# Key outputs last among the dense products, first branch-A outputs behind the attention, another deal of the sample steps

## The chip, the cores and the metric

The kernel runs on one core of one Trainium2 chip. A core has TensorE (matrix products; PE below, with PEld for its weight loads), VectorE (DVE), ScalarE (ACT), GpSimd (POOL) and SyncE (SP), which here issues DMA transfers. The engines run their own instruction lists in order and wait for one another by semaphores. The metric is the device time of one execution in microseconds. Before the change the median of three runs is 1980.49 us (1976.86 to 1985.71).

## The reference

One decoder layer is computed in float32 for two groups with shared weights: a prompt of 1024 tokens and a sample group of 8 sequences with 4 new tokens each and 8192 cached tokens in pages. The core of it:

```python
h = rmsnorm(x, g_norm1) * (1 + scale1) + shift1
za, zq, zkv, zg, zm = split(h @ w_in)              # gMLP, queries, keys/values, gates, merge gates
ya = chunk_spatial_gating(u, vn, w_spatial, b_spatial)          # u, v from gelu(za)
yb = nsa_attention(q, kv_rows, win_rows, ...)      # compressed + selected blocks + window, gated sum
gate_a, gate_b = split(sigmoid(zm))
mixed = (gate_a * (ya @ w_branch_a) + gate_b * (yb @ w_branch_b)) @ w_out
x = x + gate1 * mixed
x = x + gate2 * conv_ffn(rmsnorm(x, g_norm2) * (1 + scale2) + shift2)
```

The attention has three parts: over compressed blocks of 64 keys, over the 16 blocks that the compressed scores select, and over a window of 512 keys. The outputs are the results y of both groups, the new key and value rows (among them `o_k`, the keys of the selected and window branches), the window buffers, the normalised v rows and the rows of the convolution's state.

## The kernel before

**Numbers.** Each float32 product is made of three passes of TensorE over a high part and a low part of both operands (helper `mm`, L56; all matmuls that go through it carry this line). The parts are made by ACT (a cast, L319) and DVE (a subtraction, L320) in `split`. All columns of the layer, 1024 prompt and 32 sample tokens, stand side by side as R = 1056 columns in three chunks of 384, 384 and 288 (`CH`). `products` computes 128 output rows for one chunk: for K input tiles 3K matmuls into one PSUM bank, then an eviction.

**Stages.** Statistics of x and the tiles of h; row products; gMLP; then the dense outputs that remain, in the list `fill`: four query tiles (`query`), two key tiles (`key`; key 0 is that of the selected, key 1 of the window branch), 16 merge gates (`merge_gate`, kept in DRAM as `sig_d`). Between them stand groups of the compression of the cached pages (`compress`, 16 in all; its ACT and DVE ends are L553, L568 and L569), of which groups 14 and 15 come behind the last dense output. Tiles of 128 x 1056 live in a pool of 24 slots; h holds 16 of them until the dense outputs are done.

**The start of the attention.** `key` writes its tile to DRAM (`o_k`). `key_tiles` reads it back (L843) and makes, for each of the two heads, a high and a low part in both halves of the partitions: ACT casts (L847), DVE subtracts (L848), and DVE copies both into the other half (L849 the high, L850 the low part). `queries` makes the query parts of one tile of 128 tokens (ACT L864, DVE L865).

**The attention.** The prompt's 8 query tiles times 4 head groups are 32 units; unit n computes its scores in `attend`, the exponentials on ACT (L1136), the transposes of the probabilities on TensorE (L1161) and, two units later, `values`. The sample group's selected blocks are worked on in 32 steps between them: `sel_scores`, `sel_turn`, `sel_values`, and after every fourth step `sel_merge`, a small chain of DVE, ACT and two matmuls, which comes from `later` with a count of turns of `one_more` between its parts. Each step needs a page buffer, one of four, which SyncE fills with 16 loads of 128 KB (L522). The same four buffers take the chunks of `w_ada` (L1053; in every fourth unit) and, in two places, the weights of the near keys (L909, L911). At the end they take `ya` and `w_ba` (L1262, L1267).

**What sets the order.** Within the attention TensorE's order is the order in which the program is written (`tc.manual_schedule`), so `one_more`, `later` and the numbers that generators yield place every matmul. Other engines are ordered by the framework's scheduler. The steps are dealt to the units by `work` and `due` (L1253 and L1254): a unit's weight is an estimate of its work plus a constant, and `due[n]` is the number of steps that are to be started by unit n.

**Blocks.** `blocks` selects each sample query's compressed blocks; the part for the second group of four sequences is put on TensorE's list in unit 0. It yields the number of turns until its next part; the part behind its second yield (L794) starts with 16 small transposes of the mask, which need DVE's selection (L781 to L789).

**After the attention.** Branch A: 8 outputs, each of three products of 12 matmuls over the parts of `ya`, multiplied at the eviction (L1358) with the merge gate's tile, which SyncE loads (L1355). Their PSUM banks come from `pA`, a pool of the products; the attention uses four banks from `pM`. Then branch B, `w_out`, and the convolutional network follow.

Of the kernel before, what the change touches and what calls it, by code (L numbers as in the profile page):

```python
# [6 lines left out]
F32 = mybir.dt.float32  # L7
F32R = mybir.dt.float32r
# [3 lines left out]
OP = mybir.AluOpType  # L12
# [3 lines left out]
R = 1056  # L16
# [34 lines left out]
def step_kernel(tc, A):  # L51
# [23 lines left out]
    def pA():  # L75
        return psum([128, 512], F32, "A", 4)
# [18 lines left out]
    def slot(dt=F32):  # L95
        return S([128, R], dt, "S", NS)
# [220 lines left out]
    def split(t, hi, lo):  # L317

        act.copy(hi, t)  # L319
        dve.tensor_tensor(lo, t, hi.bitcast(F32), op=OP.subtract)  # L320
# [91 lines left out]
                lo.append(b[:, i * 128:(i + 1) * 128])  # L412
        return hi, lo

    def products(w, xh, xl, a, b, evac, behind=()):

        ps = pA()[:, 0:b - a]
        K = len(xh)
        for k in reversed(range(K)):
            with ExitStack() as queue:  # L420
                for step, ins in behind:
                    if K - 1 - k >= step:
                        queue.enter_context(tc.issue_after(ins.ins))
                mm(ps, w[0][k], xh[k][:, a:b], k == K - 1, False)
                mm(ps, w[0][k], xl[k][:, a:b], False, False)
                mm(ps, w[1][k], xh[k][:, a:b], False, k == 0)
        evac(a, b, ps)

    def dense(src, K, xh, xl, evac, load_weights=weights_t):
        w = load_weights(src, K)  # L430
        for a, b in CH:
            products(w, xh, xl, a, b, evac)
# [248 lines left out]
    def merge_gate(j, sg):  # L681
        dense(A["w_t"][10 + j], 8, hh, hl,
              lambda a, b, ps, sg=sg: act.activation(sg[:, a:b], ps, AF.Tanh, scale=0.5))  # L683
        dve.tensor_scalar(sg, sg, 0.5, 0.5, op0=OP.mult, op1=OP.add)  # L684
        stored.append(pool.dma_start(sig_d[j], sg))  # L685
        return sg
# [35 lines left out]
    def query(j):  # L722
        q = slot()
        dense(A["w_t"][4 + j], 8, hh, hl,
              lambda a, b, ps, t=q: act.mul(t[:, a:b], ps, 0.125))
        for h in range(2):
            dve.tensor_copy(QB[64 * h:64 * h + 64, :, h, :, j],
                            q[64 * h:64 * h + 64, NP:R].rearrange("p (b t) -> p b t", t=4))
        pool.dma_start(q_d[j], q)

    def key(j):
        kr = slot()
        dense(A["w_t"][8 + j], 8, hh, hl, lambda a, b, ps, t=kr: act.copy(t[:, a:b], ps))
        dve.tensor_copy(k_new[:, j], kr[:, NP:R])
        pool.dma_start(A["o_k"][j], kr)
        if j == 1:
            for b in range(8):
                pool.dma_start(A["o_wsk"][b][:, 508:512], kr[:, NP + 4 * b:NP + 4 * b + 4])
# [10 lines left out]
    def blocks(gr, bank):  # L749

        pt = bank()
        mm(pt[:, 0:24], bt_sel[0:32, gr], G[0:32, 8], True, True)
        gt = small(24, "sm24", 1).rearrange("p (a h) -> p a h", h=8)
        dve.tensor_tensor(gt, pt[:, 0:24].rearrange("p (b h) -> p b h", h=8),
                          head01[:, None, :].to_broadcast([128, 3, 8]), op=OP.mult)
        dve.tensor_reduce(GR[:, gr], gt, axis=AX.X, op=OP.add)
        g4 = small(4, "pg", 1)
        dve.tensor_scalar(g4, cg4, GR[:, gr, 1:2], None, op0=OP.mult)
        ps = bank()
        for i in range(4):  # L760
            b = 4 * gr + i
            mm(ps[32 * i:32 * i + 32, 0:128], QB[:, b].rearrange("p h t g -> p (h t g)"), kc_of(b), True, True)
        nm = small(1, "ps", 3)
        dve.tensor_reduce(nm, ps[:, 0:128], axis=AX.X, op=OP.max, negate=True)
        p = small(128, "pa", 3)
        su = small(1, "ps", 3)
        act.activation(p, ps[:, 0:128], AF.Exp, bias=nm, accum_out=su)
        r = small(1, "ps", 3)
        dve.tensor_scalar(r, su, 1e-30, None, op0=OP.max)
        dve.reciprocal(r, r)  # L770
        dve.tensor_scalar(p, p, r, None, op0=OP.mult)
        yield 3
        pt = bank()
        mm(pt[:, 0:4], rep, g4, True, True)
        dve.tensor_copy(GS[:, 4 * gr:4 * gr + 4], pt[:, 0:4])
        pt = bank()
        mm(pt[:, 0:128], grp, p, True, True)
        MA = small(128, "pa", 3)
        dve.memset(MA, 0.0)
        wk = MA[:, 1:127]  # L780
        dve.tensor_copy(wk, pt[:, 1:127])  # L781
        m8 = small(8, "m8", 2)
        dve.max(m8, wk)
        dve.match_replace(wk, m8, wk, -1.0)
        m8 = small(8, "m8", 2)
        dve.max(m8, wk)
        dve.memset(m8[:, 5:8], -5.0)
        dve.match_replace(wk, m8, wk, -1.0)
        dve.tensor_scalar(wk, wk, 0.0, NEG, op0=OP.is_ge, op1=OP.mult)  # L789
        pt = bank()  # L790
        pe.transpose(pt[:, 0:128], p, ident)
        pct = small(128, "pa", 3)
        act.copy(pct, pt[:, 0:128])
        yield 3  # L794
        pt = bank()
        for i in range(4):
            for c in range(4):
                mm(pt[32 * c:32 * c + 32, 32 * i:32 * i + 32], ident[:, 32 * i:32 * i + 32],
                   MA[:, 32 * c:32 * c + 32], True, True)
        dve.tensor_copy(MB[:, 4 * gr:4 * gr + 4], pt[:, 0:128].rearrange("p (b n) -> p b n", n=32))  # L800
        po = bank()
        for i in range(4):
            mm(po[32 * i:32 * i + 32, 0:128], pct[:, 32 * i:32 * i + 32], vc_of(4 * gr + i), True, True)
        oc = small(128, "pa", 3)
        dve.tensor_scalar(oc, po[:, 0:128], GR[:, gr, 0:1], None, op0=OP.mult)
        yield 2
        pt = bank()
        mm(pt[:, 0:128], oc, ident, True, True)
        dve.tensor_copy(YCW[:, gr], pt[:, 0:128])

    first_blocks = blocks(0, pT)

    fill = [lambda j=j: query(j) for j in range(4)] + [lambda j=j: key(j) for j in range(2)]
    fill += [lambda j=j: merge_gate(j, slot()) for j in range(16)]
    fill = iter(fill)
    R2B = new_pool("r2b")
    n = 5
# [16 lines left out]

    KH, KL = [], []

    def key_tiles(j, anchor):
        k0, k1 = slot(F32R), slot(F32R)
        l0, l1 = slot(F32R), KX([128, NP], F32R) if j else slot(F32R)
        kr = slot()  # L840
        if anchor is not None:
            dve.tensor_copy(kr[0:1, 0:1], anchor[0:1, R - 1:R])
        sync.dma_start(kr[:, 0:NP], A["o_k"][j][:, 0:NP])  # L843
        f = kr[:, 0:NP]
        for h, k, l in ((0, k0, l0), (1, k1, l1)):
            own, other = slice(64 * h, 64 * h + 64), slice(64 - 64 * h, 128 - 64 * h)
            act.copy(k[own, 0:NP], f[own])  # L847
            dve.tensor_tensor(l[own, 0:NP], f[own], k[own, 0:NP].bitcast(F32), op=OP.subtract)  # L848
            dve.tensor_copy(k[other, 0:NP], k[own, 0:NP].bitcast(F32))  # L849
            dve.tensor_copy(l[other, 0:NP], l[own, 0:NP].bitcast(F32))  # L850
        KH.append((k0, k1))
        KL.append((l0, l1))
# [13 lines left out]
        return qs  # L866


    qt = [slot() for _ in range(4)]
    for j in range(4):  # L870
        sync.dma_start(qt[j], q_d[j])
    key_tiles(0, None)
    key_tiles(1, None)
    VV = [slot(), slot()]
    for i in range(2):
        sync.dma_start(VV[i][:, 0:1024].rearrange("p (k c) -> p k c", c=256),
                       A["o_rows"][1][512 * i:512 * i + 512].rearrange("(k p) c -> p k c", p=128))

    q_first = queries(TILES[0], KL[0][0])
    for n in (14, 15):  # L880
        compress_act(*compress(n))
    compress_end()
    R2B.release()
    PG.release()
# [365 lines left out]

            later(turning(), 3)

    work = [i + 1 + min(i + 1, 5) + 6 for i, _ in units]  # L1253
    due = [max(0, 33 * sum(work[2:n + 1]) // sum(work[2:])) for n in range(len(units))] + [33] * (AHEAD + 1)  # L1254
    m = 0
    ya, ah, al = [], [], []
# [70 lines left out]
    with tc.manual_schedule(engines={mybir.EngineType.PE}):  # L1327
        later(qtile(TILES[0]), 0)
        one_more()
        for n in range(len(units) + AHEAD):  # L1330
            step(n)
        while pending:
            one_more()
    psum.release()
# [10 lines left out]


    yh, yl = [], []
    ma = []
    for m in range(8):
        w = slot(F32R)  # L1350
        split(wba[:, m], w[:, 0:512], w[:, 512:1024])
        w = [[w[:, c + 128 * k:c + 128 * k + 128] for k in range(4)] for c in (0, 512)]
        t = slot()
        dve.tensor_copy(t[0:1, 0:1], al[3].bitcast(F32)[0:1, R - 1:R])
        sync.dma_start(t, sig_d[m])  # L1355
        for a, b in CH:
            products(w, ah, al, a, b,
                     lambda a, b, ps, t=t: dve.tensor_tensor(t[:, a:b], t[:, a:b], ps, op=OP.mult))  # L1358
        ma.append(t)
    R3S.release()  # L1360
    R3.release()
    KX.release()
# [500 lines left out]
```

## Time and profile before

| | |
|---|---|
| median of the runs | 1980.49 us (1976.86, 1980.49, 1985.71) |
| profiled execution: its time | 1976.38 us |
| its span, first to last instruction | 1974.7 us |
| mean granted TensorE clock | 0.976 |
| TensorE busy | 1853.6 us |
| last dense output ends, by TensorE's row at 597.00 | 597.0 us |
| attention's first scores | 617.98 us |
| last page load issued | 995.9 us |
| branch A's first matmuls | 1019.4 us |

The profile comes from one execution. A row of the timeline has the start in us from the span's beginning, the length, the engine, the line of the kernel, the operation with its shapes, a count of instructions taken together, and in brackets the idle time of this engine ahead of it and what ended it. The granted clock is the share of TensorE's full speed that the chip's throttle allowed. SPq is SyncE's queue of DMA issues; the length there is the time of issuing, not of the transfer.

### The profile page before, as it was taken

To read this page: it belongs to the slowest core of one execution; us is meant where nothing else is said; L and a number is where in the kernel's file an instruction comes from. 1 tells how busy PE (TensorE), PEld (TensorE's weight loads), DVE (VectorE), ACT (ScalarE), POOL (GpSimd) and SP (SyncE) were. 2 spreads that over 40 slices of the span, in tenths; PEclk is the share of its full clock that TensorE was granted. 3 is DMA by queue.
4 is the path that set the end of the run, shared out by engine and by line. 5 is a ranking of instruction groups with operands and counts; after the bars stand their busy time and mean duration, and the time that the engine had idled before them with its cause. 6 is when DMAs were issued, how large, how long until landed. Compare 5 with 4: busy or idle time off the path is not lost.

```text
span 1974.7 us, 43773 instructions
## 1 busy us (share of the span) xinstructions
PE 1853.6 (94%) x16073; PEld 1746.1 (88%) x16073; DVE 1181.3 (60%) x2536; ACT 786.8 (40%) x1602; POOL 483.7 (24%) x624
## 2 busy tenths in 40 slices
PE   6799999999998998989889999799999999999996
PEld 4799999999997776767679999789999999999996
DVE  6613421112115676676665768899999999756464
ACT  4313111112114554656551357334444444545342
POOL 3410110100000000000001411766777765201010
PEclk9799999999998999999999999899999999999998
DMA  8364656766658577677773444233322223856462
GB/s 327 97 207 129 195 184 211 243 220 201 211 171 273 178 245 234 223 230 231 232 259 136 150 164 143 76 104 105 103 98 71 73 88 95 291 188 209 137 190 89
DMA packets 253894, 346.14 MB, mean 175 GB/s; under 512 B 35280, under 2 KB 189296, under 8 KB 251504
## 3 DMA queue, kind: packets, MB, share of 16 engines
q1 hardware_dynamic: 205696, 262.91, 41.3%
q10 hardware_dynamic: 36896, 41.22, 6.5%
q0 software_dynamic: 11088, 39.21, 5.6%
q8 instruction: 127, 2.08, 0.4%
q14 instruction: 87, 0.71, 0.1%
HBM read 305.96 MB, written 41.43 MB: 176 GB/s over the span
## 4 chain that ended last, share of the span: by engine, by line
PE 76%; DVE 7%; SPq 4%; issue 4%; DMA 4%; ACT 3%; POOL 1%; DVEq 0%; ACTq 0%; POOLq 0%
PE t L56 73%; SPq L522 3%; PE t L1161 2%; DMA t<-w_ada 2%; DVE t L320 1%; DMA t<-t 1%; DVE t L1583 1%; ACT t L319 1%; POOL t L1546 1%; DVE t L1523 1%; SPq L512 1%; DVE t L1522 1%; ACT t L1165 1%; PE t L991 0%; DMA t<-psel 0%
## 5 line engine op out<-in xcount | busy, mean ns | idle before, releaser
L56 PE MATMUL t<-t,t 128*128 128x264 f32 (+12 forms) x15298 | 1777.6, 306 | 91.7 <-DVE t L173 14.8
L56 PEld LDWEIGHTS t<-t,t 128*128 128x128 f32 (+3 forms) x15138 | 1663.5, 170 | 144.3 <-issue 61.3
L320 DVE TENSOR_TENSOR t<-t,t 128x512 fp32r<-128x512 f32 (+2 forms) x478 | 386.5, 817 | 324.5 <-ACT t L319 319.5
L319 ACT CAST t<-t 128x512 fp32r<-128x512 f32 (+5 forms) x544 | 311.1, 589 | 437.5 <-PE t L56 332.3
L1583 DVE TENSOR_TENSOR t<-t,t 128x264 f32<-128x264 f32 (+2 forms) x366 | 107.3, 340 | 11.8 <-PE t L56 11.7
L1192 POOL COPY t<-t 128x256 f32<-128x256 f32 x32 | 13.1, 411 | 297.1 <-DVE t L1190 185.9
L1161 PEld LDWEIGHTS t<-t,t 128*128 128x128 f32 x528 | 58.4, 144 | 30.4 <-ACT t L1010 9.2
L1521 ACT ACTIVATE t<-t,t 128x1072 f32<-128x1072 f32 x44 | 56.6, 1286 | 60.3 <-DVE t L1583 41.7
L1165 ACT COPY t<-t 128x512 f32<-128x512 f32 (+1 forms) x112 | 58.8, 568 | 46.5 <-PE t L1161 46.3
L683 ACT ACTIVATE t<-t 128x384 f32<-128x384 f32 (+1 forms) x48 | 22.2, 465 | 136.6 <-PE t L56 115.0
L1522 DVE SCALAR_TENSOR_TENSOR t<-t,t,t 128x1072 f32<-128x1072 f32 x44 | 73.2, 1663 | 5.4 <-ACT t L1521 4.6
L1161 PE MATMUL t<-t,t 128*128 128x128 f32 x528 | 74.9, 281 | 0.7 <-DVE t L1213 0.3
L1136 ACT ACTIVATE t<-t,t 128x640 f32<-128x640 f32 (+3 forms) x64 | 56.2, 878 | 37.8 <-DVE t L1135 32.4
L1706 POOL TENSOR_TENSOR t<-t,t 128x384 f32<-128x384 f32 (+1 forms) x12 | 14.9, 1274 | 228.9 <-ACT t L1764 228.9
L1523 DVE SCALAR_TENSOR_TENSOR t<-t,t,t 128x1072 f32<-128x1072 f32 x44 | 69.7, 1584 | 0.0
L1135 DVE TENSOR_REDUCE t<-t 128x1 f32<-128x640 f32 (+3 forms) x64 | 58.9, 921 | 17.9 <-PE t L56 16.1
L1546 POOL TENSOR_TENSOR t<-t,t 128x512 f32<-128x512 f32 x22 | 47.1, 2140 | 87.6 <-DMA t<-w_up 77.0
L685 POOL DMA_DIRECT2D t<-t x16 | 8.5, 532 | 220.0 <-DVE t L684 163.9
L1608 POOL TENSOR_TENSOR t<-t,t 128x1024 f32<-128x1024 f32 x22 | 54.0, 2453 | 17.3 <-ACT t L1607 17.3
L981 DVE TENSOR_TENSOR t<-t,t 128x512 f32<-128x512 f32 x32 | 22.1, 690 | 42.7 <-PE t L56 42.6
L1402 POOL TENSOR_TENSOR t<-t,t 128x384 f32<-128x384 f32 (+1 forms) x24 | 27.9, 1165 | 71.9 <-DVE t L1401 68.7
L320 DVE TENSOR_TENSOR t<-t 128x384 fp32r<-128x384 f32 (+1 forms) x66 | 36.9, 585 | 11.7 <-ACT t L319 11.5
(282 smaller groups left out, 1275.6 us busy)
## 6 DMA issues: line engine op xcount, KB each, us to landing
t<-psel SPq DMA_DIRECT2D x512, 128.0 KB
t<-pcmp SPq DMA_DIRECT2D x332, 128.0 KB
t<-w_down SPq DMA_DIRECT2D x120, 256.0 KB
t<-t POOLq DMA_DIRECT2D x50, 528.0 KB, 4.3
t<-w_up SPq DMA_DIRECT2D x96, 256.0 KB
t<-pcmp ACTq DMA_DIRECT2D x180, 128.0 KB
t<-w_ada SPq DMA_DIRECT2D x16, 1024.0 KB
t<-w_t ACTq DMA_DIRECT2D x52, 256.0 KB
```

Of the source, the lines that this page charges most:

```text
L56: return pe.matmul(out, lhsT, rhs, start=start, stop=stop)
L319: act.copy(hi, t)
L320: dve.tensor_tensor(lo, t, hi.bitcast(F32), op=OP.subtract)
L522: d = queue.dma_start(dst, src[bass.ds(r, 1)].rearrange("g p c -> p (g c)"))
L1135: dve.tensor_reduce(m4[:, branch, h:h + 1], ps[:, :, 0:w], axis=AX.XY, op=OP.max, negate=True)
L1161: pe.transpose(pt[:, c:c + 128], probs[branch, h][:, 128 * b:128 * b + 128], ident)
L1165: (act.copy if w > 2 else dve.tensor_copy)(probs[branch, h][:, 128 * k:128 * (k + w)], pt[:, c:c + 128 * w])
L1521: act.activation(acc[:, 0:w], up[:, 0:w], AF.Identity, scale=cw[:, n, 0:1], bias=cw[:, n, 3:4])
L1522: dve.scalar_tensor_tensor(acc[:, 0:w], up[:, 1:1 + w], cw[:, n, 1:2], acc[:, 0:w], op0=OP.mult, op1=OP.add)
L1523: dve.scalar_tensor_tensor(acc[:, 0:w], up[:, 2:2 + w], cw[:, n, 2:3], acc[:, 0:w], op0=OP.mult, op1=OP.add)
L1546: pool.tensor_tensor(s1, a21, a22, op=OP.add)
L1583: dve.tensor_tensor(o, by4(banks[c][:, c0:c0 + n], n), other(c, c0, n) if other else o, op=OP.add)
```

## The change

Four things are changed.

1. The list of dense outputs ends with the two keys; queries and merge gates stand ahead of them. `key` notes its tile in `kr_of`, and `key_tiles` uses that tile in place of the copy read from DRAM, so that L843 and the slot of the read tile go. The copy of the high part into the other half is now a cast by ACT from the same source; DVE's L849 goes. The key tiles are made ahead of the loads of the query tiles, and compression 14 is written ahead of the first `queries`. The stores of the keys come with the keys.
2. `blocks` yields 6 in place of 3 at its second pause.
3. The constant in `work` is 1 in place of 6. The steps 3, 7, 8, 16, 24 and 25 (counted from 0) start one unit earlier; the others stay where they were.
4. The body of branch A's loop is a function `branch_a(m, bank)`. Outputs 0 to 2 are called within the attention's written order, behind the last unit, with its banks `pM` and three turns of `one_more` behind each product; outputs 3 to 7 follow after the attention as before, with `pA`.

```diff
-    def products(w, xh, xl, a, b, evac, behind=()):
+    def products(w, xh, xl, a, b, evac, behind=(), bank=pA):
-        ps = pA()[:, 0:b - a]
+        ps = bank()[:, 0:b - a]
...
+    kr_of = []
     def key(j):
         kr = slot()
+        kr_of.append(kr)
...
-        yield 3
+        yield 6
...
-    fill = [lambda j=j: query(j) for j in range(4)] + [lambda j=j: key(j) for j in range(2)]
-    fill += [lambda j=j: merge_gate(j, slot()) for j in range(16)]
+    fill = [lambda j=j: query(j) for j in range(4)] + [lambda j=j: merge_gate(j, slot()) for j in range(16)]
+    fill += [lambda j=j: key(j) for j in range(2)]
...
-    def key_tiles(j, anchor):
+    def key_tiles(j):
         k0, k1 = slot(F32R), slot(F32R)
         l0, l1 = slot(F32R), KX([128, NP], F32R) if j else slot(F32R)
-        kr = slot()
-        if anchor is not None:
-            dve.tensor_copy(kr[0:1, 0:1], anchor[0:1, R - 1:R])
-        sync.dma_start(kr[:, 0:NP], A["o_k"][j][:, 0:NP])
-        f = kr[:, 0:NP]
+        f = kr_of[j][:, 0:NP]
         for h, k, l in ((0, k0, l0), (1, k1, l1)):
             own, other = slice(64 * h, 64 * h + 64), slice(64 - 64 * h, 128 - 64 * h)
             act.copy(k[own, 0:NP], f[own])
+            act.copy(k[other, 0:NP], f[own])
             dve.tensor_tensor(l[own, 0:NP], f[own], k[own, 0:NP].bitcast(F32), op=OP.subtract)
-            dve.tensor_copy(k[other, 0:NP], k[own, 0:NP].bitcast(F32))
             dve.tensor_copy(l[other, 0:NP], l[own, 0:NP].bitcast(F32))
...
+    key_tiles(0)
+    key_tiles(1)
     qt = [slot() for _ in range(4)]
     for j in range(4):
         sync.dma_start(qt[j], q_d[j])
-    key_tiles(0, None)
-    key_tiles(1, None)
...
+    compress_act(*compress(14))
     q_first = queries(TILES[0], KL[0][0])
-    for n in (14, 15):
-        compress_act(*compress(n))
+    compress_act(*compress(15))
...
-    work = [i + 1 + min(i + 1, 5) + 6 for i, _ in units]
+    work = [i + 1 + min(i + 1, 5) + 1 for i, _ in units]
...
         for n in range(len(units) + AHEAD):
             step(n)
+        ma = []
+
+        def branch_a(m, bank):
+            w = slot(F32R)
+            split(wba[:, m], w[:, 0:512], w[:, 512:1024])
+            w = [[w[:, c + 128 * k:c + 128 * k + 128] for k in range(4)] for c in (0, 512)]
+            t = slot()
+            dve.tensor_copy(t[0:1, 0:1], al[3].bitcast(F32)[0:1, R - 1:R])
+            sync.dma_start(t, sig_d[m])
+            for a, b in CH:
+                products(w, ah, al, a, b,
+                         lambda a, b, ps, t=t: dve.tensor_tensor(t[:, a:b], t[:, a:b], ps, op=OP.mult), bank=bank)
+                for _ in range(3):
+                    one_more()
+            ma.append(t)
+
+        for m in range(3):
+            branch_a(m, pM)
         while pending:
             one_more()
...
-    ma = []
-    for m in range(8):
-        ...
+    for m in range(3, 8):
+        branch_a(m, pA)
```

The rows below are parts of the engines' lists: line, operation, the tile written, the tiles read, and the shape of the output. DVE at the start of the attention, before; t_7385 is the first query part, t_492 and t_493 belong to the compression:

```order
L569 TENSOR_TENSOR t_493<-t_7406,t_465 64x128
L848 TENSOR_TENSOR t_7355<-t_7357,t_7353 64x1024
L849 CAST t_7353<-t_7353 64x1024
L850 CAST t_7355<-t_7355 64x1024
L848 TENSOR_TENSOR t_7369<-t_7371,t_7367 64x1024
L849 CAST t_7367<-t_7367 64x1024
L858 CAST t_7385<-t_7355 1x1
L568 TENSOR_SCALAR t_492<-t_7480,t_462 128x64
L865 TENSOR_TENSOR t_7385<-t_7345,t_7385 64x128
L850 CAST t_7370<-t_7370 64x1024
L568 TENSOR_SCALAR t_492<-t_7551,t_462 128x64
L569 TENSOR_TENSOR t_493<-t_7551,t_465 64x128
```

and with the change, where t_7136 and t_7229 are the key tiles and t_7455 the first query part:

```order
L848 TENSOR_TENSOR t_7347<-t_7136,t_7345 64x1024
L849 CAST t_7347<-t_7347 64x1024
L568 TENSOR_SCALAR t_492<-t_7384,t_462 128x64
L849 CAST t_7348<-t_7348 64x1024
L848 TENSOR_TENSOR t_7359<-t_7229,t_7357 64x1024
L857 CAST t_7455<-t_7347 1x1
L849 CAST t_7360<-t_7360 64x1024
L864 TENSOR_TENSOR t_7455<-t_7369,t_7455 64x128 x2
L568 TENSOR_SCALAR t_492<-t_7476,t_462 128x64
L568 TENSOR_SCALAR t_492<-t_7547,t_462 128x64
L569 TENSOR_TENSOR t_493<-t_7547,t_465 64x128
```

L849 of the change is L850 of before (the low part's copy). The high part's copies are gone, the key's rows read the dense output, and the ends of the compression are behind all key and query rows.

TensorE around the second group's `blocks`, before. The 32x32 row is the mask's transposes, the 32x128 row is the products with the compressed values, the 128x320 rows are prompt scores:

```order
L56 MATMUL t_7770<-t_7726,t_69 32x32 x16
L56 MATMUL t_7788<-t_493,t_7739 32x128 x4
L56 MATMUL t_7797<-t_7353,t_7385 128x320
L56 MATMUL t_7797<-t_7355,t_7385 128x320
L1201 MATMUL t_7825<-t_69,t_7662 128x128 x2
```

and with the change:

```order
L56 MATMUL t_7956<-t_7348,t_7455 128x320
L56 MATMUL t_7956<-t_76,t_72 128x128
L56 MATMUL t_7965<-t_7722,t_69 32x32 x16
L56 MATMUL t_7983<-t_493,t_7735 32x128 x4
L1160 MATMUL t_7990<-t_69,t_7744 128x128 x4
```

The transposes and the four products with them stand 44 rows further down, behind prompt scores and the values of a unit.

DVE behind the last unit, with the change. L1342 is branch A's eviction, L1034 to L1043 the last merge (L1035 to L1044 before), L320 the splitting of weights:

```order
L1342 TENSOR_TENSOR t_14260<-t_14260,t_14263 128x384
L1342 TENSOR_TENSOR t_14260<-t_14260,t_14277 128x384
L1034 RECIPROCAL t_14293<-t_14291 128x1
L1035 TENSOR_SCALAR t_14216<-t_14216,t_14293,t_3376 128x4
L1037 TENSOR_SCALAR t_13652<-t_13652,t_14216 128x128
L1039 SCALAR_TENSOR_TENSOR t_13652<-t_13835,t_14216,t_13652 128x128
L1342 TENSOR_TENSOR t_14260<-t_14260,t_14300 128x288
L1039 SCALAR_TENSOR_TENSOR t_13652<-t_14011,t_14216,t_13652 128x128
L320 TENSOR_TENSOR t_14578<-t_14143,t_14578 128x512
L1039 SCALAR_TENSOR_TENSOR t_13652<-t_14125,t_14216,t_13652 128x128
L1043 COPY t_7563<-t_14314 128x32
```

Before, the first eviction (L1358) stands behind the merge's last copy (L1044).

More of the change, by code (lines that the diff above doesn't have):

```diff
@@ L1347, in step_kernel @@
     yh, yl = [], []
-    ma = []
-    for m in range(8):
[L1350 to L1359, printed above, removed]
+    for m in range(3, 8):
+        branch_a(m, pA)
     R3S.release()
```

## The prediction

> **What bounds the kernel now.** I read the overview first: TensorE does the work.
>
> ```profile
> PE   1853.6 (94%) x16073; PEld 1746.1 (88%) x16073; DVE 1181.3 (60%) x2536; ACT 786.8 (40%) x1602; POOL 483.7 (24%) x624
> PE 76%; DVE 7%; SPq 4%; issue 4%; DMA 4%; ACT 3%; POOL 1%; DVEq 0%; ACTq 0%; POOLq 0%
> ```
>
> The change touches 597 to 1070 us alone, so next I cut that stretch into windows. The columns are the window, its length, then the busy time of PE, weight loads, DVE, ACT and POOL, the granted clock, the DMA share and GB/s.
>
> ```profile
> 612.00:617.95 5.95, 0.57 (x8) 0.43 (x8) 5.63 (x16) 1.61 (x2) 0.00 (x0) 0.90 1.10 341
> 617.95:631.20 13.25, 12.93 (x62) 8.95 (x62) 7.38 (x24) 4.97 (x13) 0.40 (x1) 0.53 0.75 226
> 639.60:644.00 4.40, 4.40 (x65) 3.78 (x67) 2.03 (x8) 2.16 (x8) 0.40 (x1) 0.61 0.71 222
> 644.00:660.70 16.70, 15.71 (x206) 12.64 (x206) 13.63 (x43) 9.60 (x25) 0.98 (x4) 1.00 0.20 62
> 662.00:995.90 333.90, 305.79 (x3612) 234.22 (x3606) 219.10 (x581) 190.43 (x515) 24.32 (x62) 0.98 0.74 233
> 1015.20:1019.10 3.90, 0.05 (x1) 0.00 (x0) 3.69 (x11) 0.30 (x1) 0.90 (x1) 1.00 1.02 418
> 1019.40:1022.90 3.50, 3.50 (x13) 3.50 (x13) 1.64 (x9) 0.00 (x0) 0.00 (x0) 0.51 1.02 399
> 1023.10:1026.60 3.50, 3.50 (x25) 3.50 (x24) 1.91 (x4) 2.43 (x4) 0.00 (x0) 1.00 1.07 383
> ```
>
> Four stretches differ. Around 612 and 1015 us TensorE is idle while DVE works (5.63 of 5.95 and 3.69 of 3.90 us). Right behind each, TensorE is busy throughout but its clock is 0.53 and 0.51: the last two rows show 13 matmuls in 3.50 us, then 25 in the next 3.50. From 662 to 995.9 us TensorE has 28.1 us of slack (333.90 less 305.79), so something else may set the pace there. SyncE's queue, read next, says what:
>
> ```profile
> 645.68 2.14 SPq L522 DMA_DIRECT2D t<-psel  x3
> 660.73 0.81 SPq L1053 DMA_DIRECT2D t<-w_ada  x2
> 662.15 25.29 SPq L522 DMA_DIRECT2D t<-psel  x35
> ...
> 963.50 32.38 SPq L522 DMA_DIRECT2D t<-psel  x48
> 995.92 0.94 SPq L1262 DMA_DIRECT2D t<-t  x2
> ```
>
> It stands still from 647.8 to 660.73 us, when a page buffer comes free, and from there on issues page loads to 995.9 us. The last rows hold three steps of 16 loads: 32.38/48 is 0.67 us a load, 10.8 us a step. I list the waits on this stretch (us in all, times, longest):
>
> ```profile
> PE t L56 <- DMA t<-psel: 9.1, 5, 3.5
> SPq L522 <- DMA t<-w_ada: 17.0, 11, 2.2
> SPq L522 <- PE t L56: 1.7, 6, 0.6
> ```
>
> SyncE waits for TensorE 1.7 us in 335 us, so the chain of page loads sets when the sample steps end. A gain ahead of 660.7 us counts if it frees that first buffer earlier.
>
> **The keys.** The waits at the start of the attention are in the timeline (start, length):
>
> ```profile
> 595.55 0.98 SPq L843 DMA_DIRECT2D t<-o_k  x2
> 597.55 0.71 DVE L684 TENSOR_SCALAR t<-t 128x1056 f32<-128x1056 f32 x1 [10.87 <-ACT t L683]
> 598.56 0.53 POOL L685 DMA_DIRECT2D t<-t  x1 [1.35 <-DMA t<-t]
> 602.41 2.11 ACT L847 CAST t<-t 64x1024 fp32r<-64x1024 f32 x2 [4.90 <-DMA t<-o_k]
> 603.49 1.22 DVE L848 TENSOR_TENSOR t<-t,t 64x1024 fp32r<-64x1024 f32 x1 [4.73 <-ACT t L847]
> 604.74 0.69 DVE L849 CAST t<-t 64x1024 fp32r<-64x1024 f32 x1
> 612.38 0.57 PE L56 MATMUL t<-t,t 128*64 128x64 f32 x8 [0.63 <-ACT t L553]
> 616.54 0.69 DVE L850 CAST t<-t 64x1024 fp32r<-64x1024 f32 x1
> 617.54 0.29 DVE L569 TENSOR_TENSOR t<-t,t 64x128 f32<-64x128 f32 x1
> 617.98 6.10 PE L56 MATMUL t<-t,t 128*128 128x320 f32 x24 [5.03 <-DVE t L569]
> ```
>
> The key tile is read back from DRAM; ACT waits 4.90 us for it, and DVE behind ACT works from 603.49 to 617.83 without a gap. TensorE has finished its compress matmuls at 612.95 and waits for the end of DVE's list (the two small instructions of the last compression, L568 and L569, stand last). The change removes the read-back: key 0 lies in SBUF from its own dense output, and the casts may start when the last dense chunk gives slots free; I take about 594.5, bounds 594.2 (SyncE's first load into such a slot, just ahead of L843) and 597.6 (the last dense output's end). DVE loses the four L849 copies, 4 x 0.69 = 2.76 us, and keeps 4 x 1.22 + 4 x 0.69. ACT gets these copies: eight casts of 1.05 (2.11/2) in place of four, 8.4 us, done by about 603 to 606; the query casts stand behind them. So DVE has its key and query work done near 607 (617.83 less 7.9 of earlier start and 2.76), well before the compression is finished. What is late next is TensorE's own compression: 612.95, then L568 and L569 (0.57 us) and a hand-over of 0.15 give 613.7. **4.2 us earlier**; bounds 0 (ACT's doubled casts, or key slots held until their stores are out) and 5.0 (the whole wait). The stores of the keys and their window rows, ten of them, now stand on POOL's queue from about 597; at 0.53 us each (L685) they take 5.3 us, and POOL has 0.40 us of work in the 13 us from 617.95: 0.
>
> **The clock behind it.** For 13.25 us TensorE is busy and runs at 0.53. If it waits 0.7 us instead of 5.03, I expect full speed. Were all of the 12.93 us array time, full speed would need 6.9 and save 6.0; but the units here also wait on reductions and exponentials that don't scale, so I take a little over half. **3.5 us**; bounds 0 and 6. In the Trainium skill, "TensorE: Matmul & The Clock Gate", Part 1, the clock falls to half after an idle window of about 3.4 us and rises again after about 3.4 us of work. The 5.03 and 3.93 us waits were followed by half clock, in agreement, and the second lasted 3.5 us; but the first took 13 us to recover, which the page's 3.4 us doesn't give: by it the gain would be 1.7 us instead of 3.5.
>
> **Second part of the compressed blocks.** Its transposes wait for DVE's selection:
>
> ```profile
> 636.53 1.03 PE L56 MATMUL t<-t,t 128*128 128x320 f32 x6
> 637.23 0.79 ACT L1136 ACTIVATE t<-t,t 128x640 f32<-128x640 f32 x1 [1.25 <-DVE t L1135]
> 639.21 0.23 DVE L789 TENSOR_SCALAR t<-t 128x126 f32<-128x126 f32 x1
> 639.58 1.76 PE L56 MATMUL t<-t,t 128*32 128x32 f32 x44 [2.02 <-DVE t L789]
> ```
>
> With the pause of 6 instead of 3, the rows after them come first; the next of those needs the exponential that ends at 638.02, so about 0.5 us of the 2.02 stays. **1.5 us** (bounds 0 and 2.0). The clock of 0.61 in 639.6 to 644 should then be whole: 4.40 us at 0.61 are 2.7 at full speed; a part of that is copies, so **1 us** (0 and 1.7).
>
> These four sum to 4.2 + 3.5 + 1.5 + 1 = 10.2 us, and move the release at 660.73 to about 650.5. The limit is 12.9 us, since SyncE is busy until 647.8 itself. The page chain then runs 10.2 us earlier, and with it the end of the attention.
>
> **The dealing of the steps.** The last constant of the work count (6 to 1) puts steps 3, 7, 8, 16, 24 and 25 one unit earlier; the loads and their bytes remain. SyncE waits for nobody, so the chain doesn't shorten: **0**. Bounds: the 9.1 us of page waits gone with one half-clock spell, −9; or the new waits of the third rival, +17.5. I take the middle since the page loads hold SyncE without a pause.
>
> **Branch A behind the last unit.** Here is the tail:
>
> ```profile
> 1014.89 0.35 PE L56 MATMUL t<-t,t 128*128 128x1 f32 x2 [0.39 <-DVE t L1030]
> 1016.47 0.14 DVE L1035 RECIPROCAL t<-t 128x1 f32<-128x1 f32 x1
> 1017.13 0.41 DVE L1036 TENSOR_SCALAR t<-t,t,t 128x4 f32<-128x4 f32 x1
> 1017.58 0.29 DVE L1038 TENSOR_SCALAR t<-t,t 128x128 f32<-128x128 f32 x1
> 1017.90 1.13 DVE L1040 SCALAR_TENSOR_TENSOR t<-t,t,t 128x128 f32<-128x128 f32 x3
> 1019.17 15.02 PE L56 MATMUL t<-t,t 128*128 128x32 f32 x82 [3.93 <-DVE t L1040]
> 1025.30 0.55 DVE L1358 TENSOR_TENSOR t<-t,t 128x384 f32<-128x384 f32 x1
> 1028.40 0.68 DVE L320 TENSOR_TENSOR t<-t,t 128x512 fp32r<-128x512 f32 x1
> ```
>
> Now the first two products stand ahead of the last merge's sum, the third ahead of its transposing matmul. Behind that matmul on TensorE stands output 1. A product is twelve matmuls, and output 0 has three, of 384, 384 and 288 columns. The fast window gives 0.14 us for a mean matmul (3.50/25, widths mixed); I take 0.16 for the wide and 0.14 for the narrow ones. On the times of before: products one and two from 1014.5 (1014.89 less its wait) to 1018.5 (24 x 0.16 and 0.1 of hand-over). DVE's order now has both evictions ahead of the reciprocal, and the third eviction and an L320 within the merge: second eviction 0.55, to 1019.1; reciprocal to the first L1040 0.14 + 0.41 + 0.29 + 0.38 (1.13/3), to 1020.4; third eviction 0.5, to 1020.9; then 0.38 + 0.68 + 0.38, to 1022.4, and 0.3 for the hand-over and the matmul: output 1 starts at 1022.7. TensorE is through with the third product at 1020.2, so a new wait of some 2.2 us stands there. Before, output 1 starts at 1019.40 + 3.50 (13 matmuls) + 23 x 0.16 = 1026.6. **3.9 us**; bounds 1.5 (the first eviction waits for its gate tile, whose loads run at a DMA share of 1.02 there, and the whole merge waits behind it on DVE) and 6 (no wait at the merge).
>
> **Sum:** 4.2 + 3.5 + 1.5 + 1 + 0 + 3.9 = 14.1 us. The profiled execution took 1976.38 us (span 1974.7) and becomes 1962.3. It lies 4.1 us below the median 1980.49, so the forecast for the median is **1966 us**.
>
> **Rivals.** *Only the tail pays:* the buffer at 660.73 comes free no earlier, since its holder waits for something that doesn't move (ACT's casts, stores), and the page chain then sets the attention's end as before. For it: 335 us of loads without a pause, which hand no later gain on; against: in the 16.70 us ahead of the release TensorE is busy for 15.71, at full clock and a DMA share of 0.20, so the release follows TensorE. It gives −3.9: 1976.6, no change.
>
> *The dealing pays too:* the five page waits (9.1 us) shrink and part of their half-clock spells: −7 more, 1959. For it: the steps are started earlier; against: a load that comes at the queue's pace can't be used before it lands.
>
> *The steps come due too early (slower):* a unit lasts 335/32 = 10.5 us, as long as a step's load, and six steps are now asked for one unit earlier. Loads come at SyncE's pace, so a step with less than 10.5 us between landing and use now waits on TensorE, and all that stands behind it in the written order waits too. If the four of steps 8, 16, 24 and 25 each wait as the longest does now, that is 4 x 3.5 = 14 us, and two half-clock spells of 1.75 (half of 3.50) make 17.5: −14.1 + 17.5 = +3.4, 1984. Against it: the waits of now at the end (3.5 the longest) would shrink in return. It decides from 14.1 us of added waits on.
>
> **How the numbers follow.** The forecast gets 0.61, only the tail 0.20, the dealing pays 0.11, too early 0.08. What a measurement of this kernel can tell from no change is about 0.5%, 9.9 us. The forecast's own range, from half of the start's terms (−9) to every upper bound (12.9 and 6, −18.9), is 1962 to 1972; about 0.07 of its 0.61 gains less than 9.9 us. Faster: 0.54 + 0.11 = 0.65. Slower by 0.5% needs 24 us of added waits: 0.05 of the last case. The same: 0.07 + 0.20 + 0.03 = 0.30. The range reaches down to 1956 (the dealing pays, with a little more) and up to 1979 (the tail alone, at its lower bound of 1.5).
>
> **What would show it.** Right: no ACT wait for o_k; TensorE's first score about 0.7 us behind its last compress matmul, at clock 1.00; the row of 44 small transposes with a wait under 1 us; the first load after SyncE's standstill near 650; unbroken page loads behind it, ending near 986; a wait of 1 to 3 us at the 128x32 matmul, with branch A at clock 1.00. Wrong: a first score that waits for ACT's casts or a DMA; SyncE with pauses between 650 and 986 (then dealing matters, and the chain is not the bound); page waits over 20 us.

## The result and the profile after

The changed kernel takes 1967.76 us (median of six runs, 1966.99 to 1972.99) against 1983.78 us (1976.86 to 1986.36) of the kernel before. The ratio is 0.9925 with a 95% interval of 0.9907 to 0.9942, so 14.9 us less (11.5 to 18.4). The forecast was 14.1 us less, a median of 1966 us.

The two profiled executions alone would mislead: their spans are 1974.7 and 1968.4 us, a difference of 6.3. Executions of one program lie apart by several us here: in one later comparison 23 runs of the kernel before went from 1975.0 to 1992.1 us, and a second trace of each kernel has spans of 1984.7 and 1961.8. So I read the traces stage by stage, and leave the whole to the timed runs.

**The start.** The timeline of the changed kernel, same columns as in the prediction (line numbers are moved by a few):

```profile
594.84 1.05 ACT L846 CAST t<-t 64x1024 fp32r<-64x1024 f32 x1
595.92 1.22 DVE L848 TENSOR_TENSOR t<-t,t 64x1024 fp32r<-64x1024 f32 x1 [9.23 <-ACT t L846]
602.62 1.04 ACT L847 CAST t<-t 64x1024 fp32r<-64x1024 f32 x1
605.13 2.39 DVE L864 TENSOR_TENSOR t<-t,t 64x128 fp32r<-64x128 f32 x8
612.93 0.57 PE L56 MATMUL t<-t,t 128*64 128x64 f32 x8 [0.63 <-ACT t L553]
613.84 0.29 DVE L569 TENSOR_TENSOR t<-t,t 64x128 f32<-64x128 f32 x1
614.28 1.99 PE L56 MATMUL t<-t,t 128*128 128x320 f32 x14 [0.78 <-DVE t L569]
```

The casts of the keys begin at 594.84, no DMA stands ahead of them, the eighth ends at 603.66 and DVE's query work at 607.52. Then DVE has nothing left to do here but the compression's two small instructions, and TensorE's wait of 5.03 us is 0.78 us.

**The clock behind it, and the page loads.** Windows of the changed kernel (window, length, busy time of PE, weight loads, DVE, ACT, POOL, granted clock, DMA share, GB/s):

```profile
614.28:623.15 8.87, 7.85 (x62) 5.20 (x62) 6.83 (x22) 4.98 (x13) 0.40 (x1) 1.00 1.03 308
1010.46:1016.77 6.31, 6.31 (x40) 6.05 (x38) 4.77 (x14) 1.10 (x3) 0.84 (x1) 1.00 0.97 389
1016.48:1019.89 3.41, 1.71 (x12) 1.48 (x11) 2.67 (x10) 0.62 (x1) 0.00 (x0) 1.00 1.03 397
1019.90:1023.31 3.41, 3.41 (x12) 3.41 (x11) 1.92 (x7) 2.02 (x4) 0.00 (x0) 0.50 0.84 302
651.10:992.50 341.40, 312.57 (x3677) 239.90 (x3668) 219.72 (x584) 191.76 (x517) 24.46 (x63) 0.97 0.74 232
```

The 62 matmuls that took 13.25 us at clock 0.53 take 8.87 us at 1.00. The timeline of TensorE behind the selection and of SyncE's queue:

```profile
630.10 0.93 PE L56 MATMUL t<-t,t 128*128 128x320 f32 x5 [0.61 <-ACT t L1135]
636.47 1.29 PE L56 MATMUL t<-t,t 128*32 128x512 f32 x8 [1.53 <-issue]
640.10 20.37 SPq L522 DMA_DIRECT2D t<-psel  x31
660.56 0.87 SPq L1052 DMA_DIRECT2D t<-w_ada  x2
664.07 9.83 SPq L522 DMA_DIRECT2D t<-psel  x16
681.12 19.12 SPq L522 DMA_DIRECT2D t<-psel  x30
```

The standstill from 647.8 to 660.73 us is gone but for 2.3 us (step 3's loads begin at 651.1, within the first SP row). Two new pauses are there, 2.6 us ahead of 664.07 and 3.4 us ahead of 681.12. Over the page loads (640 to 1000 us) SyncE now waits 8.6 us for TensorE, where the kernel before has 1.7:

```profile
SPq L522 <- PE t L56: 8.6, 10, 2.9
```

**The tail.** The last unit's sums end at 1010.5 us and the first product of branch A follows at once; the merge's matmul waits 1.70 us, and the clock is 0.50 in the 3.41 us from 1019.90:

```profile
1008.17 8.60 PE L56 MATMUL t<-t,t 128*128 128x128 f32 x72 [0.55 <-DVE t L1023]
1015.00 0.55 DVE L1342 TENSOR_TENSOR t<-t,t 128x384 f32<-128x384 f32 x1 [1.33 <-PE t L56]
1016.81 0.46 DVE L1342 TENSOR_TENSOR t<-t,t 128x288 f32<-128x288 f32 x1
1018.47 26.79 PE L56 MATMUL t<-t,t 128*128 128x32 f32 x155 [1.70 <-DVE t L1039]
```

### The profile page after: what moved, and what is told of

Read it like the earlier page. It is cut to its first block, busy times and chain, and to the rows that moved or that the text cites. A ratio compares the mean times of both kernels' runs of the same rounds, so it can differ in the third digit from the quotient of the medians.

```text
span 1968.4 us, 43754 instructions
## 1 busy us (share of the span) xinstructions
PE 1853.3 (94%) x16073; PEld 1744.9 (89%) x16073; DVE 1178.6 (60%) x2532; ACT 791.3 (40%) x1606; POOL 486.7 (25%) x624
## 4 chain that ended last, share of the span: by engine, by line
PE 80%; DVE 5%; DMA 5%; SPq 4%; issue 3%; ACT 3%; POOL 1%; DVEq 0%; ACTq 0%; POOLq 0%
PE t L56 77%; SPq L522 3%; DMA t<-w_ada 2%; PE t L1160 2%; DVE t L320 1%; DMA t<-t 1%; DMA t<-psel 1%; POOL t L1553 1%; ACT t L319 1%; PE t L990 1%; DVE t L1590 1%; DVE t L1134 0%; SPq L512 0%; DVE t L338 0%; ACT t L1135 0%
## 5 line engine op out<-in xcount | busy, mean ns | idle before, releaser
L320 DVE TENSOR_TENSOR t<-t,t 128x512 fp32r<-128x512 f32 (+2 forms) x478 | 386.4, 816 | 320.0 <-ACT t L319 315.9
L1160 PEld LDWEIGHTS t<-t,t 128*128 128x128 f32 x528 | 58.5, 145 | 32.2 <-issue 13.3
L1713 POOL TENSOR_TENSOR t<-t,t 128x384 f32<-128x384 f32 (+1 forms) x12 | 14.9, 1275 | 227.9 <-ACT t L1771 227.9
L320 DVE TENSOR_TENSOR t<-t 128x384 fp32r<-128x384 f32 (+1 forms) x66 | 37.0, 586 | 12.9 <-ACT t L319 12.8
```

The lines of the kernel that those rows point to most:

```text
L1160: pe.transpose(pt[:, c:c + 128], probs[branch, h][:, 128 * b:128 * b + 128], ident)
```

## The experiments

Two ways to read the result were open after the first trace: the prediction's sum (theory 1), and a chain of page loads that hands on only part of the start's gain, with the deal of the steps paying the rest (theory 2). After the first four runs a third came up: a deal that costs something, by its early step 3 (theory 3) or as a whole (theory 4). To compare traces I use four marks: C, the end of the last compress matmul; R, SyncE's first load behind the standstill; P, the end of the last page load; V, the end of the last unit's sums. R − C holds the start's gain, P − R the chain of page loads, and from V on the tail counts. From P to V pass 17.7 to 20.8 us in the 13 traces in which SyncE alone issues the page loads, while P itself lies anywhere from 984.2 to 1014.5 us: the attention's end follows the last page load.

**The old start.** Parts 1 and 2 of the change are taken back (against the changed kernel; the list is put in short):

```diff
-        yield 6
+        yield 3
-    fill = queries + merge gates + keys      # key_tiles reads kr_of
+    fill = queries + keys + merge gates      # key_tiles reads o_k back
```

> The changed kernel with the old start: keys early, read back from DRAM, pause of 3; the new deal of the steps and branch A in the attention's order stay. Theory 1 (the prediction's sum: start 10.2 us, deal 0, tail 3.9): 3.9 us faster than before. Theory 2 (the page chain passes only about 4 us of the start's gain on, as the changed kernel's trace looks, and the deal brings the missing 7): 11 us faster.

Measured: ratio 0.9975 (0.9961 to 0.9990), 5.0 us faster than before (2.0 to 7.7). R − C is 48.25 us, as before (47.75), P − R 335.4. Theory 1 said 3.9, theory 2 11: theory 2 is out.

**The old deal.**

```diff
-    work = [i + 1 + min(i + 1, 5) + 1 for i, _ in units]
+    work = [i + 1 + min(i + 1, 5) + 6 for i, _ in units]
```

> The changed kernel with 6 in place of 1 in the work count; the start and branch A as changed. Theory 1: 14.1 us faster than before, the same as the changed kernel. Theory 2: 8 us faster, 7 less than the changed kernel.

Measured: 0.9910 (0.9893 to 0.9926), 17.9 us faster (14.7 to 21.2). That is not less, as theory 2 had it, but rather more than theory 1's 14.1 and than the changed kernel's 14.9; the intervals of the two kernels overlap. P − R is 335.6 us here and was 341.4 in the changed kernel's trace, so the thought arose that the deal costs 3 us.

**Branch A behind the attention again.**

```diff
-        for m in range(3):
-            branch_a(m, pM)
...
-    for m in range(3, 8):
+    for m in range(8):
```

> The changed kernel with all eight branch-A outputs behind the attention again. Both theories: the 3.9 us of the tail are missing, so about 10 to 11 us faster than before; the wait at the merge's last matmul is 3.9 us again and branch A starts at half clock.

Measured: 0.9953 (0.9937 to 0.9968), 9.3 us faster (6.4 to 12.5): the tail's part is missing. The wait ahead of the merge's matmul is back in the trace, with two windows of 3.41 us at half clock behind it:

```profile
1008.66 0.35 PE L56 MATMUL t<-t,t 128*128 128x1 f32 x2 [0.39 <-DVE t L1029]
1012.94 19.27 PE L56 MATMUL t<-t,t 128*128 128x32 f32 x100 [3.93 <-DVE t L1039]
```

**The start alone.** Old deal and branch A behind the attention; only parts 1 and 2 are left (against the kernel before; the list is put in short).

```diff
-        yield 3
+        yield 6
-    fill = queries + keys + merge gates      # key_tiles reads o_k back
+    fill = queries + merge gates + keys      # key_tiles reads kr_of
```

> The kernel before with the keys last and the pause of 6 alone. Theory 1: 10.2 us faster, the release of the first page buffer at about 650 and the page loads without a pause from there to about 986. Theory 2: about 4 us faster, with pauses of SyncE behind 650 that eat some 6 us.

Measured: 0.9933 (0.9918 to 0.9949), 13.3 us faster (10.1 to 16.3). R − C is 37.54 us, 10.2 less than before; P − R 335.5 as against 335.2. So the start's gain reaches the end of the page loads whole. Theory 2 is out once more.

This kernel and the last one (branch A behind the attention, new deal) differ by the deal alone and ran on one chip: 1975.47 us with the new deal, 1971.57 with the old one. The new deal costs 3.9 us here by the medians (by the means 3.4, with an interval of 0.3 to 6.5 worked out from the twelve times). The page chains, new deal first:

```profile
650.10:990.10 340.00, 310.33 (x3713) 238.07 (x3702) 220.79 (x587) 192.45 (x521) 25.00 (x65) 0.98 0.75 233
651.40:986.90 335.50, 310.26 (x3662) 238.03 (x3655) 219.78 (x581) 191.34 (x516) 24.71 (x63) 0.97 0.74 232
```

**Does the chain of page loads set the end?** The kernel before with one more load behind each step's sixteen; what it loads is not used.

```diff
         load_pages([...], after, (), 3)
+        with tc.issue_after(starts[-1].ins):
+            sync.dma_start(R3S([128, 160], F32, "extra", 1), A["psel"][n][:, 0:160])
```

> The kernel before with one load more behind each step's sixteen, 80 KB that nobody reads (29 of them behind SyncE's standstill). At the rate of the others (0.67 us for 128 KB) one costs 0.42 us. If the chain of page loads sets the attention's end: 29 x 0.42 = 12 us slower than before. If TensorE and the engines that feed it set it, and the loads have slack: 0 to 4 us slower.

Measured: 1.0071 (1.0044 to 1.0097), 14.1 us slower (8.7 to 19.3). SyncE's queue shows the added load and its price, 0.42 us:

```profile
662.73 12.15 SPq L522 DMA_DIRECT2D t<-psel  x16
674.93 0.42 SPq L971 DMA_DIRECT2D t<-psel  x1
675.95 9.80 SPq L522 DMA_DIRECT2D t<-psel  x16
```

and the window from R to P is 18 us longer than before. This kernel:

```profile
661.30:1014.50 353.20, 315.59 (x3682) 241.61 (x3672) 220.84 (x585) 192.10 (x519) 24.71 (x64) 0.96 0.72 228
```

and the kernel before:

```profile
660.70:995.90 335.20, 307.09 (x3654) 235.43 (x3648) 219.10 (x581) 190.69 (x516) 24.71 (x63) 0.98 0.74 233
```

29 x 0.42 = 12.2 us, and the time grew by about that much (the 18 us of the two windows hold some us of the scatter between executions, below). From P to V pass 17.7 us, against 18.6 before. A load that nobody waits for makes the kernel longer, so the chain is the bound, as the prediction read it. What in the chain is paid, the queue's issuing or the bytes moved, this run doesn't separate. The expectation priced the load by its bytes, and that 0.42 came out is luck: issuing a page load of 128 KB (first row, kernel before) takes 0.33 us at the median, less than the added one of 80 KB (the three figures are the shortest, the median and the longest in ns):

```profile
L522 SPq DMA_DIRECT2D t<-psel x464: 332/333/1932, 662.1 to 995.5; - x155
L971 SPq DMA_DIRECT2D t<-psel x32: 422/423/1217, 626.6 to 1014.1; - x32
```

**A second trace of the kernel before.** No edit.

> The kernel before, for a second trace. Theory 1: 335 us from SyncE's first load after its standstill to the last page load's end, a wait of about 5 us at the first score, 7.6 us from the merge's matmul to output 1; what differs from the first trace by more than 1 us is not the change's.

Measured: 1.0005 (0.9988 to 1.0021). The first score waits 5.09 us, R − C is 47.84, P − R 338.6. R − C repeats within 0.1 us, and the page chain differs by 3.4 us between two executions of the same program. From the merge's matmul to output 1 pass 8.9 us, where 7.6 were expected: the half clock lasts two windows of 3.41 us there and one in the first trace. So the tail's marks move by more than 1 us without a change.

**Which step of the deal?** Two kernels: the changed one with step 3 alone put back, and the old deal with step 3 alone early.

```diff
     due = [max(0, ...) for n in range(len(units))] + [33] * (AHEAD + 1)
+    due[4] = 3
```

> The changed kernel with step 3 alone put back to its old unit; steps 7, 8, 16, 24 and 25 stay one unit early. Theory 3 (the early step 3 makes SyncE pause for buffers, which costs the page chain 5 to 6 us): 17 to 18 us faster than before, SyncE's pauses ahead of the loads of steps 4 and 5 are gone, and from SyncE's first load after its standstill to the end of the last page load pass 335.5 us. Theory 4 (the deal as a whole costs 3 to 4): about 15 us faster as the changed kernel, 340 us or more.

Measured: 0.9940 (0.9919 to 0.9961), 11.9 us faster. The pauses ahead of steps 4 and 5 are gone, as theory 3 said, and yet P − R is 342.5.

```diff
     work = [i + 1 + min(i + 1, 5) + 6 for i, _ in units]
     due = [max(0, ...) for n in range(len(units))] + [33] * (AHEAD + 1)
+    due[4] = 4
```

> The changed kernel with the old deal, but for step 3, which alone is one unit early. Theory 3: about 14 us faster than before, with the pauses of 2 to 4 us ahead of the loads of steps 4 and 5. Theory 4: 17 to 18 us faster, as the old deal.

Measured: 0.9942 (0.9925 to 0.9960), 11.5 us faster; the pauses of 2.8, 2.8 and 2.0 us are there, and P − R is 337.4. Theory 3 wanted the longer chain in the second kernel, and it is in the first: it falls. The intervals don't tell the two apart. Theory 4's chain of 340 us or more is there in the first kernel, but not its 17 to 18 us for the second (11.5; 7.9 to 14.9).

**The deal, once more on one chip.** The changed kernel again, and the old deal again:

> The changed kernel again, beside the old deal on one chip. Theory 1 (the deal is worth 0): within 2 us of the old deal. Theory 4 (the deal costs 3 to 4): 3 to 4 us slower than the old deal.

> The changed kernel with 6 in the work count again. Theory 1: as the changed kernel, about 15 us faster than before. Theory 4: 18 us faster.

Measured: 0.9926 (0.9903 to 0.9949) and 0.9927 (0.9906 to 0.9949), 14.7 and 14.5 us faster. Side by side the deal makes no difference here, so the 3 to 4 us of theory 4 are not in this pair. They were in the pair without the tail's part (3.9 us, above), and 17.9 against 14.9 points the same way. That the deal gains is shown by no pair; whether it costs nothing or some 4 us stays open. The windows from R to P of the two are alike. The changed kernel:

```profile
648.90:984.70 335.80, 310.38 (x3694) 238.45 (x3688) 219.94 (x586) 192.28 (x519) 24.80 (x64) 0.97 0.75 235
```

and the old deal:

```profile
653.30:989.60 336.30, 312.60 (x3690) 240.58 (x3684) 220.73 (x585) 192.39 (x519) 24.95 (x64) 0.96 0.74 232
```

The changed kernel has pauses of 2.1, 2.9 and 2.3 us ahead of steps 3, 4 and 5 as in its first trace; its chain is 5.6 us shorter all the same. So these pauses are not what made the first trace's 341.4 us. What did isn't settled. Chains of 340 us and more stand in three of the five traces in which steps 7, 8, 16, 24 and 25 are early (341.4, 340.0 and 342.5, against 335.8 and 335.4), and in none of the seven others with one queue and no added load (335.0 to 338.6). That points at these steps, but no run changes them alone.

**The pause in the selection.** The old deal with the pause of 3:

```diff
-        yield 6
+        yield 3
```

> The old deal with the pause of 3 in place of 6. By the prediction's terms 2.5 us slower than the old deal (1.5 for the wait, 1 for the clock behind it); if a wait of 2 us is taken back by the page chain, no difference.

Measured: 0.9922 (0.9900 to 0.9943), 15.5 us faster, on one chip with the old deal's 14.5: no difference by time. In the trace the wait is there again:

```profile
628.48 1.57 PE L56 MATMUL t<-t,t 128*32 128x32 f32 x45 [2.02 <-DVE t L792]
635.48 1.29 PE L56 MATMUL t<-t,t 128*32 128x512 f32 x8 [1.53 <-issue]
```

R − C is 38.83 us against 37.55: the pause of 6 is worth 1.3 us at this place. No half clock follows the wait here: the clock's windows of 3.41 us (last section) lie so that the wait falls across a border, with 2.17 and 2.62 us of work in the two windows.

**Page loads on two queues.** The old deal, with every fourth group of four page loads issued by ACT.

```diff
-                   after, (), 3)
+                   after, (3, 7), 3)
```

> The changed kernel with the old deal, and a quarter of the page loads issued by ACT instead of SyncE. If the queue sets the pace of the page loads, as the prediction held: the chain shrinks by up to a quarter, the page waits of TensorE vanish and the attention gets shorter by part of TensorE's 28 us of slack: 25 us or more faster than before. If the DMA engines set the pace, or ACT's work is held up by its loads' waits: no faster than the 18 us of the old deal, or less.

Measured: 1.0032 (1.0013 to 1.0052), 6.3 us slower than before. The waits of SyncE and of TensorE in the attention:

```profile
SPq L522 <- PE t L56: 58.1, 16, 5.4
PE t L990 <- ACT t L983: 21.6, 12, 5.6
PE t L56 <- ACT t L1135: 5.2, 9, 1.7
```

TensorE waits for no page any more, and SyncE waits 58.1 us for TensorE: the page loads are no longer the bound. TensorE waits for ACT instead, whose exponentials are late (21.6 us; 9.5 for the same lines of the kernel before from 660 to 1000 us). ACT's own instructions now wait 34.4 us for page loads, which they never do in the kernel before, since the loads that ACT issues stand among them in its list. The two longest:

```profile
ACT t L1164 <- DMA t<-psel: 17.2, 8, 7.0
ACT t L983 <- DMA t<-psel: 8.5, 2, 5.5
```

That a second queue moves pages faster was therefore not tested; only that ACT isn't the engine to issue them.

No kernel of these is shown to beat the changed one.

## Why the prediction was right

The marks of the traces that decide, in us. The last column is from V to the start of output 2 of branch A.

| kernel | wait at first score | first score to first transposes | R − C | P − R | V to output 2 |
|---|---|---|---|---|---|
| before | 5.03 | 13.22 | 47.75 | 335.2 | 18.12 |
| before, second trace | 5.09 | 13.01 | 47.84 | 338.6 | 19.35 |
| start alone | 0.77 | 8.86 | 37.54 | 335.5 | 18.10 |
| old start | 5.49 | 12.98 | 48.25 | 335.4 | 14.05 |
| changed | 0.78 | 8.87 | 37.60 | 341.4 | 15.59 |
| changed, second trace | 0.77 | 8.87 | 37.55 | 335.8 | 15.56 |
| changed with the old deal, second trace | 0.77 | 8.86 | 37.55 | 336.3 | 14.02 |

**The keys** (forecast 4.2 us). 5.03 became 0.78: 4.25. The steps on the way came as written: casts from 594.84 (594.5), ACT done at 603.66 (603 to 606), DVE at 607.52 (near 607), the compression last. The ten stores on POOL are issued by 609.2 us and hold nothing back.

**The clock behind it** (3.5). 13.22 became 8.87: 4.35, at clock 1.00. More of that stretch than I took scales with TensorE; the mechanism held.

**The second part of the blocks** (1.5, and 1 for its clock). From the first transposes to R pass 29.5 us before and 28.0 after (651.10 less 623.15): 1.6 in place of 2.5. A pause of 0.61 us stays, as forecast (0.5). By the run with the pause of 3 the pause is worth 1.3 us. What was mis-sized is the clock's term: in that run the same 2.02 us wait is followed by no half clock, so it is not the wait alone that costs the clock, and yet first transposes to R take 29.2 us, only 0.3 less than before. What full clock gains there goes into a wait of 1.53 us, for which the profile shows no releaser; it stands at 636.47 in the changed kernel and in every kernel with the new start, and is 0.28 in the kernel before.

**Their sum** was 10.2 and R − C fell by 10.15. The steps' errors, +0.9 and −0.9, cancel; that the sum came out so near is luck.

**The page chain hands it on.** P − R is 335.2 and 338.6 before. Behind the new start it is 335.0 to 337.4 in the five traces without the early steps 7, 8, 16, 24 and 25, and 335.8, 340.0, 341.4 and 342.5 with them. Timed, the start alone gives 13.3 us (10.1 to 16.3), which holds 10.2. The rival that only the tail pays gave no change, and is refuted by this run; the extra load shows why the chain matters. The prediction's "SyncE waits for nobody" passes over a row that it shows, 17.0 us of waits for `w_ada`; with the change they are 16.8, so nothing hangs on it here. The mark "the last page load ends near 986" came out at 992.5 in the first trace and 984.7 in the second.

**The deal** (0). The size is about right, the reason is not. The prediction put the term at nothing because the page loads hold SyncE without a pause; in the changed kernel SyncE waits 8.6 us (second trace 7.1) for TensorE, so the mark "unbroken page loads" failed and the sign of being wrong, pauses of SyncE, is there. TensorE's page waits stay far below 20 us (10.1 and 6.7). By time the pair with the tail's part has 14.7 against 14.5 us, the pair without it 9.3 against 13.3. That the deal pays 7 us is refuted, and that it costs 17.5 too; a cost between nothing and some 4 us is left open.

**The tail** (3.9). Output 1 starts 8.16 us after V in place of 12.31: 4.15 us, with a new wait of 1.70 at the merge (2.2 forecast; DVE's small instructions took 0.16, 0.29, 0.28 and 0.35, less than before). But the mark "branch A at clock 1.00" was wrong in the changed kernel's trace: the clock is 0.50 for one window behind the wait, which takes 1.6 us, and at output 2 only 2.5 us are left (15.59 against 18.12). In the old deal's second trace that window runs at full clock, and 4.1 are left. The kernel before varies as well (18.12, 19.35), so 2.5 to 5.3 us, around the forecast. Timed on one chip with the old deal, with and without the tail's part: 17.9 against 13.3 us, 4.6.

**The whole:** 14.1 us forecast, 14.9 (11.5 to 18.4) measured, and the start's 10.15 with the tail's 2.5 to 5.3 make 12.7 to 15.5 from the traces, if the page chain keeps its length. In the first trace it didn't: 10.15 less the 6.2 us by which P − R is longer there, and 2.5 of the tail, make 6.5, about the 6.3 by which the two profiled spans differ. The runs by part were larger than the forecast, too: start alone 13.3 and tail 4.6, 17.9 together, which the new deal's 3.9 in the same runs would bring back to 14.0. If that cost is real, the nearness of the total is in part errors that cancel. Setting the sum on the profiled execution's own time, and the forecast on the median of the runs, mattered: that execution (1976.38) was faster than all but two of the timed ones.

## What to carry to other kernels

Look in the profile for the queue that hardly waits for anybody, and ask of each gain whether it lets that queue start earlier; here a gain ahead of its start counted in full, and a new deal of the work that the queue feeds gained nothing and may have cost some us. A stall on TensorE can cost its own length and the slow clock behind it, and at the start here the second was as large as the first; work that is ready can be written into the stall. Where executions of one program differ by more than the change, compare marks within the traces and take the total from many runs.

## What the runs showed of the hardware

The granted clock changes on a grid of 3.41 us, and a window need not be idle to bring half clock in the next. The two pairs of windows show it, of the kernel before and of the changed kernel with the old deal (second trace):

```profile
637.20:640.61 3.41, 1.39 (x45) 0.98 (x45) 2.91 (x14) 1.77 (x4) 0.00 (x0) 1.00 0.72 225
640.62:644.03 3.41, 3.41 (x26) 2.98 (x26) 1.34 (x5) 1.95 (x6) 0.40 (x1) 0.50 0.67 207
```

```profile
1015.20:1018.61 3.41, 1.99 (x12) 1.99 (x13) 2.77 (x12) 0.38 (x1) 0.00 (x0) 1.00 1.01 377
1018.62:1022.03 3.41, 3.41 (x23) 3.41 (x22) 2.06 (x6) 2.03 (x4) 0.00 (x0) 1.00 0.84 277
```

With 1.39 us of work in a window, after a wait of 2.02, the next is slow. With 1.71 (the changed kernel's 1016.48 to 1019.89 above) it is slow too, and with 1.99 behind a wait just as long (1.69) it isn't. I counted all windows at full clock from 600 to 1060 us in 14 traces: with TensorE busy below 0.40 of the window, the next was at half clock in 48 of 48; from 0.40 to 0.45 in 8 of 11; from 0.45 to 0.55 in 12 of 43; above in 7 of 1669. The prediction compared waits with the 3.4 us of the Trainium skill ("TensorE: Matmul & The Clock Gate", Part 1), which speaks of an idle window; the measurement decides: a wait of 1.7 to 2.0 us can be enough when it falls within one window, and whether it does varies from one execution to the next. That is also where one of the marks that failed, the clock of branch A, comes from.
